# A hybrid decoder layer on one core: mask product in the scores' type, held small products, and the state decode's first part moved

## The chip, the core and the metric

The kernel runs on one core of one Trainium2 chip. The metric is the device time of one execution in microseconds (us). A core has five engines that run at the same time, each through its own queue in order: TensorE (PE, matrix products into PSUM; its weight loads are listed apart as PEld), VectorE (DVE), ScalarE (ACT), GpSimd (POOL) and SyncE (SP, which here issues nearly all DMAs). They wait for one another through semaphores.

## What is computed

One layer, for a prompt of 1024 tokens and for eight decode samples of one token each, with shared weights (width 1024). All arrays are float32.

```
h = x + 0.5 * post1(SwiGLU1(pre1(x)))                 # hidden width 2816
P = pre2(h) @ w_in                                    # 1536 columns group A, 1792 group B
group A: differential attention, 4 heads, 2 maps x 64, causal; samples attend over 512 cached tokens
group B: RWKV-7, 8 heads, state 64 x 64 (value x key) per head
    s = s*w + (s @ -kk)[:, None]*(kk*a) + v[:, None]*k ;  y = s @ r
h = h + post2(concat(A, B) @ w_out)
h = h + 0.5 * post3(SwiGLU2(pre3(h)))
```

Beside the new hidden rows it returns the keys and values, the last projected row and the new RWKV-7 states of prompt and samples. For a sample, group B is a single step of the formula, from a state that comes in (`state_wkv`, 8 samples x 8 heads x 64 x 64).

## The kernel before

**Precision.** A float32 product is made of three products in the rounded type `float32r` (`FR` in the code), which pass the array once: high part by high part, high by low, low by high (`mm3`, line 685). The trunk, the projections, the output product and attention's scores use it. Everything smaller (jobs, decode, probabilities times values, norm sums) is plain float32, which passes the array four times and shows as two matmul records a product; transposes are products with an identity. The causal mask is a third kind: a bfloat16 product `identb` x `negb` (attend, line 265) added to the diagonal block of each score tile, 0 below the diagonal and -1e30 above.

**Phases and halves.** The prompt is cut in two halves of 512 tokens, the samples ride with the first. The trunk (`s_trunk`, line 1021) has four phases: 0 and 1 are the first feed-forward of either half, 2 and 3 the second. Phases 0 and 3 use a scheme with seven block products in place of eight for most of their hidden tiles; phases 1 and 2 (`WIDE`) use 512-column products, except for their first and last hidden tile, which go in chunks of 256 (line 1202: gate and up of chunk 0, then of chunk 1). Each phase ends with down products whose sums DVE adds up (`down`, tile `trunk_xl`).

Between the feed-forwards lies the mixing of each half: projection (`s_project`), RWKV-7 jobs (`s_job`, four a half in two lanes), rotary embedding, attention (`s_prepare`, `s_attend`, `s_finish`; 16 blocks of 128 queries a half in two lanes), output product (`s_out`), norms (`s_stats`, `s_pre`). The mixing of the first half runs beside trunk phase 1, that of the second beside phase 2, so that trunk products fill PE while the mixing waits on DVE and ACT. Phase 3 needs the second half's mixing complete.

**Decode.** `s_decode_a` (1941) does the samples' attention over cached pages, `s_decode_b` (1955) their RWKV-7 step. Both live, one after the other, in one large buffer with the tag `dreg`, which phase 2's first activations use in between and the second half's attention takes over afterwards: `s_mix` (1547) of half 1 waits for the signals of its jobs, of its rotary embedding and for `dec_b`, before `a_buffers`. The trunk's phase 2 waits for `dec_a`. `b_decode` (1993) has a first part (mixing of the eight columns, decay, gates, keys, then a transpose and a store of five row vectors to the DRAM tile `Dd`) and a loop over four pairs of heads: two state loads, then five row tiles, each loaded by two DMAs that broadcast 64-float rows over 64 partitions, products and sums with the state, two state stores. A ring of three row tiles is used.

**Who orders the work.** The body is a set of generators (streams) whose operations are recorded with a price (`price`, 384) and a list of what they depend on. `run` (481) then places them: for each engine it looks at the head of each stream's queue, takes those that could start first, and among them the one with the earliest due time. The order found is written out as the program's order on every engine. The build does this eight times dry, each time with due times that come from the plan before (`latest`, 574), takes the plan with the shortest predicted time and emits it. So an edit of a price, of a rule in `run`, or of one stream gives a new order everywhere. All operations are issued from the one line 323, so the profile's lines don't tell them apart; tiles do. A tile's name begins with its stream: `trunk_`, `proj_`, `job_`, `attn_`, `prep_`, `dec_` and `decb_` for decode, `out_` or `outb_`, `outn_`, `stats_`, `pre_`, `wts_` for the feed-forward's weights, `lin_` for the other weights.

Of the kernel before, what the change touches and what calls it, by code (L numbers as in the profile page):

```python
# [14 lines left out]
FR = mybir.dt.float32r  # L15
# [83 lines left out]
SWAP = 0  # L99
# [6 lines left out]
STARVE = 1  # L106
HUNGER = 0.1
# [108 lines left out]
class Kern:  # L216
# [264 lines left out]
    def run(self):  # L481
        free, held = self.free, self.held
        table, turn = "exp", None
# [4 lines left out]
        while self.streams:  # L488
# [7 lines left out]
            for e in ENGINES:  # L496
                c = []
                for st in self.streams:
                    if st.q[e] and not st.q[e][0].left:
                        o = st.q[e][0]  # L500
                        c.append((max(free[e], o.ready + o.load, held[OTHER[e]] if o.port else lanes[0] if o.dma and e != "gpsimd" else 0.0), st.prio[e] if o.late is None else o.late, o))
                if e == "tensor":
                    starved = not c
                if c:
# [4 lines left out]
                    s, p, o = min((x for x in c if x[0] <= t), key=lambda x: (-round(x[2].columns / x[2].cost / 1000) if dense else self.feeds(x[2]) if hungry else 0, x[1], x[0]))  # L509
# [10 lines left out]
            if o.table is not None and o.table != table:  # L520
                table = o.table
                s += 1.3
            if o.eng == "tensor":
# [41 lines left out]
        self.predicted = max(free.values())  # L565

# [125 lines left out]
    def setup(self):  # L692
# [3 lines left out]
        self.identb = self.T(c, [P, P], "identb", BF)  # L696
# [95 lines left out]
    def stats(self, src, rb, tmp=("sqs", 1), **kw):  # L792

        for k in range(KT):
            if SQP:
                self.square_sum(rb, src[k], k, self.ps2()[:, :rb.shape[-1]], engines=("vector",))
            else:
                self.square_sum(rb, src[k], k, self.tmp(*tmp, rb.shape[-1]), **kw)
# [222 lines left out]
    def s_trunk(self):  # L1021
# [3 lines left out]
        for ph in range(4):  # L1025
# [160 lines left out]
            for gi, grp in enumerate(groups):  # L1186
                for q, f in enumerate(grp):
# [14 lines left out]
                    for fn, c in (((gate, 0), (up, 0), (gate, 1), (up, 1)) if f in (0, NF - 1) else  # L1202
# [46 lines left out]
    def s_tail(self, ph, c, acc, y):  # L1249
# [29 lines left out]
        if ph < 2:  # L1279
# [13 lines left out]
            self.stats(y, self.prb[:, o:o + n], ("sq", 2))  # L1293
# [288 lines left out]
    def b_setup(self, pool):  # L1582
# [6 lines left out]
        self.negb = self.T(c, [P, P], "negb", BF)  # L1589
# [77 lines left out]
    def job(self, pool, i, s, jb):  # L1667
# [143 lines left out]
        for cg in range(4):  # L1811
            nc.sync.dma_start(LT[32 * cg:32 * cg + 32], src)
# [128 lines left out]
    def s_decode_a(self):  # L1941
# [4 lines left out]
        if SWAP:  # L1946
            yield ("wait", "decb")
        yield from self.a_decode()
        if SWAP:
            self.signal("dec_b")  # L1950
        else:
            self.spawn(self.s_decode_b(), "decb", 1, "dec", ahead=8)
        self.signal("dec_a")

    def s_decode_b(self):
        yield ("wait", "proj0")
        yield ("wait", "lead2")
        if SWAP:
            yield ("wait", "setup")
            yield ("wait", "lead1")  # L1960
        take = self.arena(self.T(self.pool, [P, W_DEC], "dreg"))
        yield from self.b_decode(take, take, take(TD, C))
        self.signal("decb" if SWAP else "dec_b")

# [28 lines left out]
    def b_decode(self, m0, m1, tmp):  # L1993
# [3 lines left out]
        ring = [m0(TD, C) for _ in range(3)]  # L1997
        S = m0(TD, C)
        N32 = lambda: m1(4, TD)
        bc = lambda ap: ap.unsqueeze(2).broadcast_to([P, ap.shape[1], TD])  # L2000
        f = lambda ap: ap.rearrange("p i n -> p (i n)")
        X, xt = m1(NB, TD), m1(NB, TD)
# [11 lines left out]
        DV = m1(5, 4, TD)  # L2014
        a, g, t = N32(), N32(), N32()
# [16 lines left out]
        kk, sq = N32(), N32()  # L2032
# [16 lines left out]
        bv = N32()  # L2049
# [5 lines left out]
        V.tensor_tensor(f(bv), f(v), ps[:, :32], ALU.mult)  # L2055

        dv = DV.rearrange("p w i n -> p (w i n)")
        for o, w in ((0, P), (P, 32)):
# [4 lines left out]
            nc.sync.dma_start(self.Dd[o:o + w, :], dr[:w])  # L2063
        yield
        y, sa = N32(), m1(TD)
        at = 0
        kb = lambda ap: ap.unsqueeze(2).broadcast_to([P, TD, C])

        def rows(w, i):
            nonlocal at  # L2070
            B = ring[at % 3]
            at += 1
            for h in range(2):
                src = self.Dd[w * 32 + i * TD:w * 32 + (i + 1) * TD, 64 * h:64 * h + 64]
                nc.sync.dma_start(B[64 * h:64 * h + 64], src.unsqueeze(0).broadcast_to([64, TD, C]))
            return B

        for i in range(4):
            for h in range(2):
                nc.sync.dma_start(S[64 * h:64 * h + 64], I["state_wkv"][0, :, 2 * i + h].rearrange("n v k -> v n k"))  # L2080
            B = [rows(w, i) for w in range(3)]
            yield
            V.tensor_tensor(tmp, S, B[0], ALU.mult)
            B.append(rows(3, i))
            V.tensor_reduce(sa, tmp, AX.X, ALU.add)
            G.tensor_tensor(S, S, B[1], ALU.mult)
            B.append(rows(4, i))
            yield
            V.tensor_tensor(tmp, B[2], kb(sa), ALU.mult)
            V.tensor_tensor(S, S, tmp, ALU.add)  # L2090
            yield
            V.tensor_tensor(tmp, B[3], kb(v[:, i, :]), ALU.mult)
            V.tensor_tensor(S, S, tmp, ALU.add)
            for h in range(2):
                nc.sync.dma_start(self.O[7][0, :, 2 * i + h].rearrange("n v k -> v n k"), S[64 * h:64 * h + 64])
            V.tensor_tensor(tmp, S, B[4], ALU.mult)
            V.tensor_reduce(y[:, i, :], tmp, AX.X, ALU.add)
# [122 lines left out]
    def s_prepare(self, pool, half):  # L2220
# [5 lines left out]
        for rd in range(4 * half, 4 * half + 4):  # L2226
# [121 lines left out]
    def a_decode(self):  # L2348
# [12 lines left out]
        m0, m1 = self.arena(reg[:, 4 * HS + 4 * W:]), self.arena(more)  # L2361
# [162 lines left out]
def hymba_kernel(ctx, tc, I, O, late=None, dry=False):  # L2524
# [10 lines left out]
    K.Dd = DR([160, P], "Dd")  # L2535
# [3 lines left out]
    K.drams = {t.tensor.name: (tuple(t.shape), []) for t in (K.res, K.PTall, K.YMall, *K.Md, *K.Xd, K.Dd, K.Qd, O[3], *K.Ld, *K.Lg, K.Li, K.Lo)}  # L2539
# [27 lines left out]
    if SWAP:  # L2567
        K.spawn(K.s_decode_b(), "decb", 1, "dec", ahead=8)
# [11 lines left out]
_OUTS = [(P, KT, HS), (P, KT, TD), (26, P, NT), (1, 1, TP, 4, P), (P, 4, C), (HS, D), (P, 4, TD), (1, 8, 8, 64, 64)]  # L2580


def layout(inputs):

    f = lambda n: np.asarray(inputs[n])
    given = {n: f(n) for n in _INS if n in ("x_prompt", "cache_k", "cache_v", "state_wkv", "page_table", "w2", "a2", "g2", "ffn1_down", "ffn2_down") or n.startswith("lambda")}
# [5 lines left out]
    for n in ("ffn1_gate", "ffn1_up", "ffn2_gate", "ffn2_up", "w_in", "w_out"):  # L2592
        given[n] = f(n)[0].reshape(KT, P, -1, P).transpose(2, 1, 0, 3)
    given["consts"] = const_table()
# [3 lines left out]
def natural(o):  # L2598
# [8 lines left out]
           ks.transpose(2, 1, 0)[None, :, None], heads(pt[8:12, :, SAMPLE])[None, :, None], states, shift(pt[12:, :, SAMPLE])[None])  # L2607
# [30 lines left out]
```

## Time and profile before

| | us |
|---|---|
| three runs | 2263.15, 2260.83, 2264.13 (median 2263.15) |
| profiled execution, whole | 2263.6 |
| profiled execution, span of its instructions | 2261.8 |
| PE busy | 2204.0 |
| DVE, ACT, POOL busy | 1561.4, 1078.3, 983.4 |

The mean granted clock of PE was 0.994 of full speed. The page lists groups of instructions as `out<-in`. In a timeline row stand the start, the time from the first start to the last end, the engine, the operation, the shapes and the count; in brackets the engine's idle time before it and what ended that. A matmul's listed duration includes its passage through the array, so matmuls overlap; what one costs in a dense stretch is the distance from its start to the next start. In the busy time by stretches, PEclk is the clock granted to PE.

### The profile page before, as it was taken

The page shows a single profiled execution, that of the slowest core. Times are in us where ns is not written, and L with a number is a line of the kernel's source. Part 1 is how long each engine was busy: PE and PEld are TensorE (multiplying, and loading weights), DVE is VectorE, ACT ScalarE, POOL GpSimd, SP SyncE. Part 2 cuts the span into 40 slices and gives each one's busy share as a digit, 9 for nine tenths or more (in the row PEclk, how much of TensorE's full clock was granted, in tenths as well). Part 3 has the DMA queues.
Part 4 walks back from the last instruction along what each step waited for, and adds up shares of the span by engine and source line. Part 5 has one row for each costly group of instructions (what it writes and reads, how often), then busy time and mean ns, then how long its engine had stood idle before and what let it go on. Part 6 is the DMA issues. An engine that isn't in the chain of part 4 may idle for free. (4 is left out here: it accounts for less than half of the span.)

```text
span 2261.8 us, 42336 instructions
## 1 busy us (share of the span) xinstructions
PE 2204.0 (97%) x15671; PEld 1961.9 (87%) x15671; DVE 1561.4 (69%) x3583; ACT 1078.3 (48%) x2222; POOL 983.4 (43%) x817
## 2 busy tenths in 40 slices
PE   8999998999999999999999999999999998999998
PEld 8999998898887777988887777778888988999998
DVE  7758887746766677478656767666877455777775
ACT  6524443644553455343554445333665465544344
POOL 3525554533233575365544334132543254444443
PEclk9999999999999999999999999999999998999999
DMA  7322233444343666555454435358634856443443
GB/s 261 109 94 94 85 103 113 139 148 128 102 121 107 197 185 196 193 177 164 153 197 153 141 94 154 105 146 217 196 108 135 288 175 240 138 135 107 142 141 112
DMA packets 241768, 338.76 MB, mean 150 GB/s; under 512 B 78938, under 2 KB 160282, under 8 KB 241562
## 3 DMA queue, kind: packets, MB, share of 16 engines
q1 hardware_dynamic: 241274, 335.53, 47.3%
q8 instruction: 124, 2.03, 0.4%
q14 instruction: 82, 0.67, 0.1%
q10 hardware_dynamic: 288, 0.52, 0.1%
HBM read 281.01 MB, written 54.98 MB: 149 GB/s over the span
## 5 line engine op out<-in xcount | busy, mean ns | idle before, releaser
L323 PE MATMUL trunk_m<-trunk_xl,wts_w 128*128 128x256 f32 (+2 forms) x2604 | 433.7, 318 | 14.5 <-DVE trunk_xl L323 11.9
L323 PE MATMUL trunk_m<-pre_X,wts_w 128*128 128x512 f32 (+3 forms) x2400 | 430.2, 333 | 9.3 <-ACT wts_w L323 6.5
L323 POOL TENSOR_TENSOR wts_w<-wts_raw,wts_w 128x1024 fp32r<-128x1024 f32 (+2 forms) x154 | 291.9, 1902 | 331.1 <-ACT wts_w L323 284.4
L323 PEld LDWEIGHTS trunk_m<-trunk_xl,wts_w 128*128 128x128 f32 x2604 | 366.2, 190 | 44.4 <-DVE trunk_xl L323 13.5
L323 PEld LDWEIGHTS trunk_m<-pre_X,wts_w 128*128 128x128 f32 x2400 | 353.1, 190 | 49.7 <-ACT wts_w L323 5.9
L323 PE MATMUL trunk_m<-pre_T,wts_w 128*128 128x512 f32 (+3 forms) x1848 | 358.2, 346 | 6.0 <-DVE trunk_xl L323 4.4
L323 ACT CAST wts_w<-wts_raw 128x1024 fp32r<-128x1024 f32 (+3 forms) x299 | 244.9, 834 | 239.7 <-PE trunk_m L323 159.2
L323 PE MATMUL proj_m<-tail_xl,lin_w 128*128 128x256 f32 (+2 forms) x1920 | 327.2, 323 | 0.4 <-POOL lin_w L323 0.4
L323 PEld LDWEIGHTS trunk_m<-pre_T,wts_w 128*128 128x128 f32 x1848 | 288.0, 191 | 43.7 <-issue 2.7
L323 PEld LDWEIGHTS proj_m<-tail_xl,lin_w 128*128 128x128 f32 x1920 | 269.7, 188 | 36.6 <-issue 11.5
L323 DVE TENSOR_TENSOR trunk_xl<-trunk_xl,trunk_m 128x256 f32<-128x256 f32 (+2 forms) x351 | 165.9, 490 | 59.3 <-PE trunk_m L323 57.9
L323 POOL TENSOR_TENSOR lin_w<-lin_raw,lin_w 128x1024 fp32r<-128x1024 f32 x44 | 106.2, 2414 | 199.5 <-ACT lin_w L323 161.7
L323 POOL TENSOR_TENSOR trunk_xl<-trunk_t,trunk_xl 128x512 fp32r<-128x512 f32 (+3 forms) x85 | 92.0, 1084 | 188.3 <-ACT trunk_xl L323 184.7
L323 DVE TENSOR_TENSOR wts_w<-wts_raw,wts_w 128x1024 fp32r<-128x1024 f32 (+3 forms) x115 | 115.7, 1011 | 20.4 <-ACT wts_w L323 18.1
L323 ACT CAST lin_w<-lin_raw 128x1024 fp32r<-128x1024 f32 x52 | 54.5, 1047 | 80.3 <-PE proj_m L323 48.1
L323 ACT CAST wts_w<-wts_lraw 128x512 fp32r<-128x512 f32 x94 | 55.7, 619 | 64.6 <-DMA wts_lraw<-in_ffn_down_dram 36.0
L323 DVE TENSOR_TENSOR trunk_t<-trunk_g,trunk_m 128x512 f32<-128x512 f32 (+2 forms) x75 | 41.9, 559 | 54.0 <-PE trunk_m L323 51.7
L323 PE MATMUL trunk_aux<-trunk_xl,wts_w 128*128 128x256 f32 (+1 forms) x516 | 71.3, 283 | 0.0
L323 PE MATMUL trunk_m<-comb_T,wts_w 128*128 128x260 f32 x540 | 69.7, 283 | 0.0
L323 POOL TENSOR_TENSOR wts_w<-wts_lraw,wts_w 128x512 fp32r<-128x512 f32 x39 | 54.1, 1390 | 35.7 <-ACT wts_w L323 32.3
L323 ACT CAST wts_w<-wts_dec 128x512 fp32r<-128x512 f32 x30 | 17.6, 587 | 107.0 <-DVE wts_dec L323 107.0
L323 PEld LDWEIGHTS trunk_m<-comb_T,wts_w 128*128 128x128 f32 x540 | 66.9, 188 | 0.0
(612 smaller groups left out, 4091.5 us busy)
## 6 DMA issues: line engine op xcount, KB each, us to landing
wts_raw<-in_ffn_gate_dram SPq DMA_DIRECT2D x87, 512.0 KB
wts_raw<-in_ffn_up_dram SPq DMA_DIRECT2D x58, 512.0 KB
lin_raw<-in_w_in_dram SPq DMA_DIRECT2D x52, 512.0 KB
wts_raw<-in_ffn_down_dram SPq DMA_DIRECT2D x56, 384.0 KB
wts_raw<-in_ffn_down_dram SPq DMA_DIRECT2D x29, 512.0 KB
wts_w<-Ld SPq DMA_DIRECT2D x22, 512.0 KB
mix_T<-out_dram SPq DMA_DIRECT2D x36, 256.0 KB
Ld<-wts_w SPq DMA_DIRECT2D x24, 384.0 KB
```

Of the source, the lines that this page charges most:

```text
L323: o = Op(eng, lambda: fn(*a, **k), st)
```

## The change

1. **Mask.** `identb` and `negb` become `float32r`, the type of the scores' products.
2. **Held products.** `price` marks products that pass the array once (`table`; one of `float32r` or bfloat16). In `run`, when the last product was of the one-pass kind, at least one candidate is of that kind and exactly one candidate is not, that one's earliest start is put to 0.5 us after it is ready (`HOLD`). In the planner's timeline a one-pass product that follows another kind in an array of the same shape costs 0.085 us more (`MODE`). `STICK` is 0 and adds nothing.
3. **State decode.** The first part becomes a stream of its own, `decf`, spawned where the attention decode begins and free to run once the first projection is done; it lives in the unused end of `dreg`. It stores gate, bonus term and value to a new DRAM tile `Ed`. `dec_a` waits for it. The second part loads `Ed`, asks for up to four row tiles ahead, and each row tile comes by one DMA in runs of 512 floats (2 KB), since `Dd` is now laid out by half. States are laid out on the host so that they come and go in single DMAs of contiguous rows.
4. **Smaller edits.** Norm sums of phases 2 and 3 square into `E` in place of a buffer `sqs`. The first hidden tile of phases 1 and 2 uses 512-column products. The job's solve matrix and attention's raw keys and queries are loaded by one broadcast DMA in place of four and two.

The core of the diff:

```diff
+HOLD = 0.5
+MODE = 0.085
+STICK = 0
...
+            o.table = f == 1
...
+                if e == "tensor" and HOLD and round_ and any(x[2].table for x in c) and sum(not x[2].table for x in c) == 1:
+                    c = [x if x[2].table else (max(x[0], x[2].ready + HOLD), *x[1:]) for x in c]
...
+                if o.table and not round_:
+                    o.cost += MODE * (size == (t[1] - t[0], t[3] - t[2]))
+                round_ = o.table
...
-        self.identb = self.T(c, [P, P], "identb", BF)
+        self.identb = self.T(c, [P, P], "identb", FR)
-        self.negb = self.T(c, [P, P], "negb", BF)
+        self.negb = self.T(c, [P, P], "negb", FR)
...
-                    for fn, c in (((gate, 0), (up, 0), (gate, 1), (up, 1)) if f in (0, NF - 1) else
+                    for fn, c in (((gate, 0), (up, 0), (gate, 1), (up, 1)) if f == NF - 1 or f == 0 and not wide else
...
-            self.stats(self.staged[c], self.own[c][2][:, :n])
+            self.stats(self.staged[c], self.own[c][2][:, :n], self.E[:, W * c:W * c + n])
...
-        for cg in range(4):
-            nc.sync.dma_start(LT[32 * cg:32 * cg + 32], src)
+        nc.sync.dma_start(LT, src.unsqueeze(0).broadcast_to([4, 32, 1024]))
...
-                    for q in range(2):
-                        nc.sync.dma_start(raw[64 * q:64 * q + 64], src(4 * w + h, t0)[64 * j:64 * j + 64])
+                    nc.sync.dma_start(raw, src(4 * w + h, t0)[64 * j:64 * j + 64].unsqueeze(0).broadcast_to([2, 64, HS]))
```

And the state decode:

```diff
         yield from self.a_decode()
-            self.spawn(self.s_decode_b(), "decb", 1, "dec", ahead=8)
+        yield ("wait", "dec_f")
+        self.spawn(self.s_decode_b(), "decb", 1, "dec", ahead=16)
         self.signal("dec_a")
+    def s_decode_f(self, m0, m1):
+        yield ("wait", "proj0")
+        yield from self.f_decode(m0, m1)
+        self.signal("dec_f")
...
+        V.tensor_copy(gbv[:, 2], v)
+        nc.sync.dma_start(self.Ed, gbv.rearrange("p w i n -> p (w i n)"))
...
-            nc.sync.dma_start(self.Dd[o:o + w, :], dr[:w])
+            nc.sync.dma_start(self.Dd[:, o:o + w, :].rearrange("h p k -> p h k"), dr[:w].rearrange("p (h k) -> p h k", h=2))
...
+        def ask(upto):
+            nonlocal asked
+            while asked < min(upto, 20):
+                i, w = divmod(asked, 5)
+                if w == 0:
+                    nc.sync.dma_start(both[i % 2].rearrange("p n k -> p (n k)"), I["states"][i])
+                B = ring[asked % 4].rearrange("p n k -> p (n k)")
+                src = self.Dd[:, w * 32 + i * TD:w * 32 + (i + 1) * TD, :].rearrange("h n k -> h (n k)")
+                nc.sync.dma_start(B, src.unsqueeze(1).broadcast_to([2, 64, TD * C]))
+                asked += 1
+        ask(4)
...
-            for h in range(2):
-                nc.sync.dma_start(self.O[7][0, :, 2 * i + h].rearrange("n v k -> v n k"), S[64 * h:64 * h + 64])
+            nc.sync.dma_start(self.O[7][i], S.rearrange("p n k -> p (n k)"))
...
+        self.spawn(self.s_decode_f(self.arena(reg[:, at + 512:]), self.arena(more[:, 260:])), "decf", 1, "dec", ahead=8)
```

More of the change, by code (lines that the diff above doesn't have):

```diff
@@ L482, in run @@
         free, held = self.free, self.held
[L483 removed]
+        table, turn, round_ = "exp", None, True
         last = self.last = {}
@@ L508, in run @@
                     hungry = STARVE and starved and e in ("vector", "scalar")
-                    s, p, o = min((x for x in c if x[0] <= t), key=lambda x: (-round(x[2].columns / x[2].cost / 1000) if dense else self.feeds(x[2]) if hungry else 0, x[1], x[0]))
+                    s, p, o = min((x for x in c if x[0] <= t), key=lambda x: (-round(x[2].columns / x[2].cost / 1000) if dense else self.feeds(x[2]) if hungry else 0,
+                                                                              x[1] + STICK * (e == "tensor" and (x[2].table != round_ or self.shape(x[2].tile) != size)), x[0]))
                     if e == "tensor":
@@ L519, in run @@
             self.backlog[o.eng] -= o.cost
-            if o.table is not None and o.table != table:
+            if o.eng == "scalar" and o.table is not None and o.table != table:
                 table = o.table
@@ L565, in run, with shape @@
         self.predicted = max(free.values())
+    @staticmethod
+    def shape(t):
+        return t[1] - t[0], t[3] - t[2]
     @staticmethod
@@ L2062, in b_decode @@
             self.copy(dr[:w], ps[:w, :P])
-            nc.sync.dma_start(self.Dd[o:o + w, :], dr[:w])
+            nc.sync.dma_start(self.Dd[:, o:o + w, :].rearrange("h p k -> p h k"), dr[:w].rearrange("p (h k) -> p h k", h=2))
         yield
-        y, sa = N32(), m1(TD)
-        at = 0
-        kb = lambda ap: ap.unsqueeze(2).broadcast_to([P, TD, C])
[L2069 to L2072, printed above, removed]
-            for h in range(2):
-                src = self.Dd[w * 32 + i * TD:w * 32 + (i + 1) * TD, 64 * h:64 * h + 64]
-                nc.sync.dma_start(B[64 * h:64 * h + 64], src.unsqueeze(0).broadcast_to([64, TD, C]))
-            return B
+    def b_decode(self, take):
+        nc, I = self.nc, self.I
+        V, A, G, mm = nc.vector, nc.scalar, nc.gpsimd, nc.tensor.matmul
+        bc = lambda ap: ap.unsqueeze(2).broadcast_to([P, ap.shape[1], TD])
+        f = lambda ap: ap.rearrange("p i n -> p (i n)")
+        kb = lambda ap: ap.unsqueeze(2).broadcast_to([P, TD, C])
+        ring = [take(TD, C) for _ in range(4)]
+        both = [take(TD, C) for _ in range(2)]
+        tmp, gbv, y, sq, sa = take(TD, C), take(3, 4, TD), take(4, TD), take(4, TD), take(TD)
+        g, bv, v = (gbv[:, j] for j in range(3))
+        nc.sync.dma_start(gbv.rearrange("p w i n -> p (w i n)"), self.Ed)
+        asked = 0
+        def ask(upto):
[9 more added lines that the diff above has]
+        ask(4)
+        yield
@@ L2078, in b_decode @@
         for i in range(4):
[L2079 to L2082, printed above, removed]
+            S = both[i % 2]
+            B = [ring[(5 * i + w) % 4] for w in range(5)]
             V.tensor_tensor(tmp, S, B[0], ALU.mult)
-            B.append(rows(3, i))
+            ask(5 * i + 5)
             V.tensor_reduce(sa, tmp, AX.X, ALU.add)
@@ L2538, in hymba_kernel @@
     K.Li, K.Lo = DR([26, P, KT, P], "Li"), DR([KT, P, KT, P], "Lo")
-    K.drams = {t.tensor.name: (tuple(t.shape), []) for t in (K.res, K.PTall, K.YMall, *K.Md, *K.Xd, K.Dd, K.Qd, O[3], *K.Ld, *K.Lg, K.Li, K.Lo)}
+    K.drams = {t.tensor.name: (tuple(t.shape), []) for t in (K.res, K.PTall, K.YMall, *K.Md, *K.Xd, K.Dd, K.Ed, K.Qd, O[3], *K.Ld, *K.Lg, K.Li, K.Lo)}
     K.c2 = K.const
@@ L2593, in layout @@
         given[n] = f(n)[0].reshape(KT, P, -1, P).transpose(2, 1, 0, 3)
+    given["states"] = f("state_wkv")[0].reshape(TD, 4, P, C).transpose(1, 2, 0, 3).reshape(4, P, TD * C)
     given["consts"] = const_table()
```

58 lines of the change are left out of this document (24 added, 34 removed).

## The prediction

> **What bounds the kernel now.** I read the page first, then the busy time by stretches, then the timeline of each stretch in which TensorE (PE) is not full.
>
> ```profile
> span 2261.8 us, 42336 instructions
> ## 1 busy us (share of the span) xinstructions
> PE 2204.0 (97%) x15671; PEld 1961.9 (87%) x15671; DVE 1561.4 (69%) x3583; ACT 1078.3 (48%) x2222; POOL 983.4 (43%) x817
> ```
>
> PE is busy 97% of the span and every other engine 69% or less, so what counts is work removed from PE or idle time removed on PE. Of idle time there are only 2261.8 - 2204.0 = 57.8 us. This profiled execution took 2263.6 us (its span and 1.8 us around it), 0.45 us more than the median 2263.15 of the three runs shown. My sum is made against 2263.6 and ends 0.45 lower for the median. About 0.2%, 4.5 us, is what a measurement of this kernel can tell from no change.
>
> ```profile
> core 0: us, PE busy (x) PEld busy (x) DVE busy (x) ACT busy (x) POOL busy (x), PEclk, DMA share, GB/s
> 372.00:396.00 24.00, 18.80 (x128) 18.30 (x127) 13.86 (x34) 9.76 (x21) 11.72 (x13) 0.86 0.15 44
> 1110.00:1165.00 55.00, 53.03 (x301) 45.74 (x301) 41.31 (x63) 32.76 (x63) 36.05 (x39) 1.00 0.61 210
> 1530.00:1580.00 50.00, 50.00 (x217) 40.10 (x217) 31.87 (x45) 15.08 (x18) 16.09 (x9) 1.00 0.89 222
> 1580.00:1760.00 180.00, 178.29 (x986) 147.76 (x985) 132.44 (x284) 111.93 (x299) 76.10 (x46) 1.00 0.50 150
> 1760.00:1836.00 76.00, 75.99 (x511) 69.65 (x509) 31.21 (x44) 38.38 (x65) 28.59 (x30) 1.00 0.84 286
> 1836.00:1890.00 54.00, 40.36 (x293) 37.40 (x292) 35.80 (x68) 33.36 (x66) 28.52 (x41) 0.91 0.36 112
> ```
>
> The rows are where the trunk passes from phase 0 to 1, from 1 to 2, and four pieces of the second half's mixing ahead of phase 3. One stretch stands out: 1836 to 1890, where PE has 40.36 of 54 us, 13.6 us idle, and a granted clock of 0.91. It is the largest single piece of the 57.8 us, and it is the joint between phases 2 and 3.
>
> **Why that joint is empty, and what fills it.** In the second half the trunk of phase 2 is PE's filler while the mixing runs: jobs, then attention, then the output product, then the norms that make phase 3's input.
>
> ```profile
> 1526.18 1.02 PE L323 MATMUL job_aux<-bset_sg,bset_g 128*128 128x512 f32 x2
> ...
> 1582.82 0.48 PE L323 MATMUL attn_aux<-mix_T 128*128 128x320 f32 x2
> ```
>
> The last job's last product is at 1526, attention's first at 1583. In between PE is full (50.00 of 50), but with filler alone. What holds attention is the state decode (`decb`), whose tile attention's buffers take over:
>
> ```profile
> L323 SPq DMA_DIRECT2D decb_dreg<-Dd x40: 573/628/1772, 1490.7 to 1562.1; - x40
> L323 DVE TENSOR_TENSOR decb_dreg<-decb_dreg x34: 184/690/2729, 1457.0 to 1580.2; 128x512 f32<-128x512 f32 x24, 128x32 f32<-128x32 f32 x9, 128x112 f32<-128x112 f32 x1
> ...
> L323 DVE TENSOR_REDUCE decb_dreg<-decb_dreg x8: 677/686/687, 1498.6 to 1570.3; 128x8 f32<-128x512 f32 x8
> ```
>
> It starts at 1457, loads its first row at 1490.7, loops until 1571 and ends at 1580. The filler burnt in that gap is missing at the end:
>
> ```profile
> 1832.10 2.76 PE L323 MATMUL outb_m<-outb_T,lin_w 128*128 128x256 f32 x22
> ```
> ```profile
> 1870.59 0.48 DVE L323 SCALAR_TENSOR_TENSOR pre_T<-pre_sq,init_cols,pre_T 128x256 fp32r<-128x256 f32 x1 [0.29 <-ACT pre_T L323]
> ...
> 1872.51 7.48 PE L323 MATMUL trunk_m<-trunk_xl,wts_w 128*128 128x256 f32 x45 [7.14 <-DVE trunk_xl L323]
> ```
>
> The output product ends at 1835, and the norms behind it keep DVE and ACT until 1871: a chain of 36 us. In it the trunk is already in its last down products, whose sums wait on DVE behind those norms, so PE waits 7.14 us at a stretch. After that wait 45 products of 256 columns take 7.48 us, 166 ns each, against 120 ns at 773 us (below): 2.0 us more at the lower clock. The Trainium skill (TensorE: Matmul & The Clock Gate, part 1) says that PE's clock falls to half after an idle window of some 3.4 us; the 7.14 us wait and the 0.91 agree.
>
> **The change part by part.**
>
> *State decode.* Its first part (from the load of the eight columns to the rows' store to DRAM, 1457 to 1490) moves ahead of the first half's attention, into 740 to 800 us. Every instruction of it still counts, but PE fills the place it leaves with trunk products, so this is zero in sum; it adds two small DMAs (store and reload of gate, bonus and value) and one small copy, and its few issues on SP pass between the loads of cached pages, which have slack there as decode of attention is waited for only at phase 2's start. Its result is due some 300 us later, so the new wait for it stands in nobody's way. The second part then starts where the first part starts now: 34 us earlier. Its loop takes (1571 - 1491) = 80 us for 20 rows of 256 KB, four states in and four out, 7.3 MB. With one issue a row in place of two (628 ns each, 40 to 20: 12.6 us of SP) and 2 KB packets, its bytes at the 222 GB/s of 1530:1580 take 33 us; DVE's 32 large operations, at 0.69 us, take 22. So the loop takes 33 to 80 us; I take 50. Decode's end then is 1457 + 50 + 10 = 1517, at the worst 1547, and attention is let go by the last job at 1527 or by 1547: 33 to 50 us earlier than 1580. SP may stand at a row's issue until DVE frees one of four buffers, with the trunk's weight loads queued behind it; the same waits stand there now with three buffers, so I count nothing.
>
> *What that is worth.* Filler worth 33 to 50 us is left for the 36 us chain. If all is covered, the joint is left with what a joint without such a chain has: 24 - 18.80 = 5.2 us idle at phase 0 to 1, or 55 - 53.03 = 2.0 at 1 to 2. I take the larger, since phase 2's tail has the same DVE sums. Gain at full cover: 13.6 - 5.2 + 2.0 = 10.4 us.
>
> *Small products wait for company.* When the last product was one of the trunk's kind, a trunk product is at hand, and exactly one small product stands ready, it may be put up to 0.5 us later, and its followers (DVE and ACT of that job or block) with it. This is an order fixed when the kernel is built: on the chip PE waits for no clock, it does trunk products meanwhile. First, what a change of kind costs on PE, together with the mask:
>
> ```profile
> 770.39 0.22 PE L323 MATMUL attn_aux<-mix_X 128*128 128x128 f32 x1
> 770.45 2.77 PE L323 MATMUL trunk_m<-trunk_xl,wts_w 128*128 128x512 f32 x11
> 773.06 0.28 PE L323 MATMUL attn_aux<-mix_X 128*128 128x256 f32 x1
> 773.18 0.22 PE L323 MATMUL attn_aux<-mix_X,mix_X 128*128 128x128 f32 x1
> ...
> 773.60 0.23 PE L323 MATMUL attn_aux<-bset_negb,init_identb 128*128 128x128 bf16 x1
> 773.64 0.36 PE L323 MATMUL attn_m<-mix_X 128*128 128x256 f32 x1
> 773.84 2.02 PE L323 MATMUL trunk_m<-trunk_xl,wts_w 128*128 128x512 f32 x8
> ...
> 780.46 0.60 PE L323 MATMUL prep_cb<-init_ident,mix_T 128*128 128x128 f32 x4
> 780.81 2.58 PE L323 MATMUL trunk_m<-trunk_xl,wts_w 128*128 128x512 f32 x10
> 783.23 4.33 PE L323 MATMUL trunk_m<-pre_T,wts_w 128*128 128x512 f32 x18
> ```
>
> I read starts, not durations. Four transposes take 780.81 - 780.46 = 0.35 us, and the ten trunk products behind them 2.42 in place of 10 x 0.233 = 2.33: 0.44 in all, 0.11 a transpose. The 0.09 seen on the first trunk product is what the last transpose's slot lacks (0.35 is three slots and a bit); I see no charge for the change of kind beyond it, so a merge of two groups of full-array products saves nothing. Where the array shape changes too, merging may save some; I have no row for a count, and bound all of it between 0 and 4 us (40 merges at 0.1), taking 0. The Trainium skill (TensorEngine Tiling (Array Packing), Key Properties) says that a change of tiling mode drains TensorE; by it the saving would be nearer 4.
>
> The price is in the chains. A job's chunk steps follow one another:
>
> ```profile
> 1497.93 0.40 PE L323 MATMUL job_aux<-bset_Sd,mix_T 128*128 128x128 f32 x2
> ...
> 1500.25 0.38 PE L323 MATMUL job_aux<-bset_Sd,mix_T 128*128 128x128 f32 x2
> ```
>
> One step is 2.3 us, and the wait can make it 2.8. By the code a lane has two jobs with some 25 such returns to PE each, and attention eight blocks a lane with five: 90 returns at 0 to 0.5 us, 0 to 45 us. Often two lanes stand ready or the product was no hurry; I take 15 us. So attention and output end some 45 - 15 = 30 us earlier in place of 45, and cover 30 of the 36 us: gain about 8.5 us instead of 10.4.
>
> *Mask.* The bf16 mask at 773.60 holds the array 0.04 us, and the 256-column product behind it takes 0.20 in place of the 0.12 from 773.06 to 773.18: 0.12 in all. The 128-column product of the scores' dtype at 770.39 takes 0.06, and the eleven behind it 2.61 in place of 11 x 0.233 = 2.56: 0.11 in all. So 64 masks (32 blocks, two maps each) save 64 x 0.01 = 0.6 us; bounds -1 and +4. The Trainium skill (same page as above, Fast Weight Load) speaks against it: weights of 128 columns load fast unless they are FP32. By an estimate from its column rule (128/1.2 ns at half saved, 53 ns) 64 masks would cost 3.4 us more if nothing hid the loads.
>
> *First products of phases 1 and 2 in 512 columns.* Now gate and up go in two chunks, and a bank is wanted every 2.8 us:
>
> ```profile
> 386.10 3.06 PE L323 MATMUL trunk_m<-pre_T,wts_w 128*128 128x256 f32 x24
> ...
> 391.18 5.07 PE L323 MATMUL trunk_m<-pre_T,wts_w 128*128 128x256 f32 x28 [2.02 <-DVE trunk_xl L323]
> ```
>
> After one chunk (24 products) PE waits 2.02 us for DVE to empty the other bank. A 512-column product chain runs 24 x 0.233 = 5.6 us before it wants that bank, past 391.18, so these 2.0 us go. At phase 2 no such wait is listed: 0.
>
> *The rest, at nothing.* One broadcast load for two or four (job solve, attention's raw loads) takes issues off SP, which PE waits for nowhere in these rows; if it waited, they would gain. Squares into `E` in place of their one buffer: ACT has the cover of 48% use. Every order is planned anew; I allow 3 us each way.
>
> *Sum.* 8.5 + 0.6 + 2.0 = 11.1; 2263.6 - 11.1 = 2252.5, the median 0.45 lower: **2252 us**.
>
> **The rivals.**
>
> *Held products lengthen the chains past what decode gives (slower).* If each of the 90 returns pays 0.5 us, 45 us eat the whole lead; with decode's end at 1547 (33 us) the output would end 12 us later than now. From the point where the wait adds more than decode gives, each us is one more at the joint, since the filler runs out before: 12 - 2.6 = 9.4 us, 2263.15 + 9.4 = 2272.5. For it: the last job's steps have PE to themselves, one small product at a time. Against: two lanes run for most of the time. Chance 0.11.
>
> *The joint stays as it is (no difference).* The 7.14 us wait is on the trunk's own sums on DVE, and the transposes of the rows and the blocks for phase 3 still fall there. Then only 0.6 and 2.0 are gained: 2260.5. For it: 372:396 has 5.2 us idle with no mixing about. Chance 0.16.
>
> *A change of kind costs what it seems to.* If the 0.09 on the first trunk product is a real charge, and a quarter of the returns by the code (8 jobs x 25 and 32 blocks x 5, 360) is merged, 90 x 0.09 = 8 us more go: 2244. The starts above speak against it. Chance 0.12.
>
> *The packets do nothing.* If decode's loop keeps its 80 us, its first part still leaves: that is the 1547 above, within the forecast.
>
> **How the numbers follow.** The forecast (2245 to 2258) has 0.61. The range takes in full cover, 4 us of merges, 3 of re-planning and most of the third rival (down to 2241), and the second rival with 3 us (2264); left out are the first rival and the third's edge, under 0.2. Faster by over 0.2% (below 2258.6): 0.61 + 0.12 and none of the rest, 0.73. Within: 0.16. Slower: 0.11.
>
> **What would show it.** Right: `decb` with its first row before 1460 and its end before 1530 (or the last job's end as the gate), attention's first product by 1550, the stretch between output's end and phase 3's first product with under 7 us idle and a clock near 1, no wait at 389, mask slots as before. Wrong: attention no earlier, or the output no earlier because job steps went from 2.3 to 2.8 us; or an unchanged 7 us wait for DVE at the joint; or a PE busy sum that fell by over 5 us, which would mean that changes of kind cost something.

## The result, and the profile after

The changed kernel takes 2498.62 us (median of four runs, 2497.67 to 2500.14) against 2263.64 for the kernel before on the same chip: a ratio of 1.104 with an interval of [1.102, 1.106]. It is 235 us slower; 2252 had been forecast. The page of its profile begins:

```profile
span 2497.2 us, 41941 instructions
## 1 busy us (share of the span) xinstructions
PE 2258.1 (90%) x15575; PEld 2010.0 (80%) x15575; DVE 1538.5 (62%) x3576; ACT 1078.7 (43%) x2219; POOL 993.1 (40%) x820
```

PE does about the same products and was idle for 239.1 us in place of 57.8. Its busy time rose too, by 54, at a mean granted clock of 0.948 where it had 0.994, and 181 + 54 is the whole difference of the spans. The busy time by stretches of the changed kernel says where (columns as before: the five engines, PE's granted clock, DMA share, GB/s):

```profile
700.00:1000.00 300.00, 236.70 (x1252) 190.82 (x1249) 172.66 (x453) 111.24 (x286) 120.99 (x82) 0.88 0.43 130
1400.00:1900.00 500.00, 367.75 (x2081) 292.22 (x2080) 224.88 (x637) 169.66 (x399) 135.36 (x86) 0.84 0.33 103
1664.00:1670.00 6.00, 4.75 (x19) 3.59 (x17) 0.09 (x1) 0.41 (x2) 4.63 (x3) 0.80 0.13 50
1796.00:1799.00 3.00, 3.00 (x15) 2.48 (x14) 2.17 (x6) 1.80 (x5) 1.05 (x1) 1.00 0.13 52
```

And of the kernel before, the same two long stretches:

```profile
700.00:1000.00 300.00, 293.45 (x1712) 242.79 (x1712) 200.15 (x442) 141.60 (x332) 165.58 (x120) 1.00 0.60 182
1400.00:1900.00 500.00, 481.30 (x2946) 403.03 (x2945) 320.35 (x671) 256.18 (x564) 194.06 (x159) 0.99 0.58 172
```

In the mixing of either half PE loses 63.3 and 132.3 us where it lost 6.6 and 18.7, and runs at 0.88 and 0.84 of full clock. No other engine is busier, and the DMA engines are less busy than before. The two short rows point at the loads: for microseconds on end the DMA share is 0.13, two engines of sixteen, at some 50 GB/s. In those moments only one kind of transfer is under way. SP's timeline in the state decode:

```profile
1555.27 0.33 SPq L325 DMA_DIRECT2D decb_dreg<-Ed  x1
1555.63 0.43 SPq L325 DMA_DIRECT2D decb_dreg<-in_states_dram  x1
1556.11 9.45 SPq L325 DMA_DIRECT2D decb_dreg<-Dd  x4
1565.66 5.07 SPq L325 DMA_DIRECT2D wts_raw<-in_ffn_up_dram  x1
1570.83 0.68 SPq L325 DMA_DIRECT2D decb_dreg<-Dd  x1
1571.56 6.21 SPq L325 DMA_DIRECT2D decb_dreg<-in_states_dram  x1
1577.87 0.59 SPq L325 DMA_DIRECT2D decb_dreg<-Dd  x1
1578.51 5.22 SPq L325 DMA_DIRECT2D wts_raw<-in_ffn_down_dram  x1
```

Row loads of 256 KB follow each other, and soon every other issue, of whatever load comes next, stands for 5 to 6 us: 256 KB at 50 GB/s are 5.2 us. The trunk's own weight loads (`wts_raw`) stand in that line. The same in the groups of issues by tile (ns: shortest, median, longest), the changed kernel first, then the kernel before:

```profile
L325 DVE TENSOR_TENSOR decb_dreg<-decb_dreg x28: 185/692/696, 1563.7 to 1698.8; 128x512 f32<-128x512 f32 x24, 128x32 f32<-128x32 f32 x4
L325 SPq DMA_DIRECT2D decb_dreg<-Dd x20: 507/1254/5629, 1556.1 to 1663.1; - x20
...
L325 SPq DMA_DIRECT2D bset_la<-out_dram x11: 532/4126/6326, 764.3 to 1863.7; - x11
```
```profile
L323 SPq DMA_DIRECT2D bset_la<-out_dram x20: 422/567/597, 728.1 to 1663.9; - x20
```

Fewer issues, but the median one takes 4.1 us in place of 0.57. The waits of the changed kernel (us in total, times, longest):

```profile
DVE decb_dreg L325 <- DMA decb_dreg<-Dd: 68.8, 15, 7.3
...
ACT mix_T L325 <- DMA mix_T<-out_dram: 48.7, 11, 5.6
...
PE job_aux L325 <- ACT mix_T L325: 34.8, 7, 10.4
```

The first two are row tiles and raw tiles. PE's own wait at the jobs hangs on both, since DVE and ACT take their work in order. Two of its seven waits in the timeline:

```profile
1677.70 0.69 DVE L325 TENSOR_TENSOR decb_dreg<-decb_dreg 128x512 f32<-128x512 f32 x1 [5.03 <-DMA decb_dreg<-Dd]
1678.31 0.34 DVE L325 SCALAR_TENSOR_TENSOR bset_Sd<-job_aux,job_ec,init_bones 128x128 f32<-128x128 f32 x1
...
1678.69 0.42 ACT L325 COPY mix_T<-job_aux 64x64 f32<-64x64 f32 x2 [14.14 <-DVE bset_Sd L325]
...
1679.17 0.80 PE L325 MATMUL job_aux<-bset_Sd,mix_T 128*128 128x128 f32 x2 [10.42 <-ACT mix_T L325]
...
1694.81 0.62 ACT L325 CAST mix_T<-bset_la 128x512 fp32r<-128x512 f32 x1 [4.57 <-DMA bset_la<-out_dram]
1695.45 0.43 ACT L325 COPY mix_T<-job_aux 64x64 f32<-64x64 f32 x2
...
1695.93 0.80 PE L325 MATMUL job_aux<-bset_Sd,mix_T 128*128 128x128 f32 x2 [8.35 <-ACT mix_T L325]
```

At 1677 the job's step on DVE (`bset_Sd`) stands behind a row tile, at 1694 its copy on ACT stands behind a raw tile, and PE waits 10.4 and 8.4 us for them. The decode, by the first line of the groups above, ends at 1699 (before: 1580). On PE's timeline attention's first product of half 1 follows at 1724 (1583) and the output's last ones at 2041 to 2044 (1835):

```profile
1724.21 0.76 PE L325 MATMUL attn_aux<-mix_T 128*128 128x320 f32 x2 [3.27 <-ACT mix_T L325]
...
2041.40 2.77 PE L325 MATMUL outb_m<-outb_T,lin_w 128*128 128x256 f32 x22
```

**Theory.** The loads that became "one broadcast load in place of two or four" have an outermost count of 2 (rows, raws: `[2, 64, ...]`) or 4 (solve: `[4, 32, 1024]`), and run on that many DMA engines. A rival: held products and the new order stretch the chains.

### The profile page after: what moved, and what is told of

Read it like the earlier page. It is cut to its first block, busy times and chain, and to the rows that moved or that the text cites. A ratio compares the mean times of both kernels' runs of the same rounds, so it can differ in the third digit from the quotient of the medians.

```text
span 2497.2 us, 41941 instructions
## 1 busy us (share of the span) xinstructions
PE 2258.1 (90%) x15575; PEld 2010.0 (80%) x15575; DVE 1538.5 (62%) x3576; ACT 1078.7 (43%) x2219; POOL 993.1 (40%) x820
## 3 DMA queue, kind: packets, MB, share of 16 engines
q8 instruction: 123, 2.02, 0.3%
## 5 line engine op out<-in xcount | busy, mean ns | idle before, releaser
L325 PE MATMUL trunk_m<-pre_X,wts_w 128*128 128x512 f32 (+3 forms) x2352 | 439.8, 342 | 11.4 <-ACT wts_w L325 6.0
L325 PEld LDWEIGHTS trunk_m<-pre_X,wts_w 128*128 128x128 f32 x2352 | 359.9, 194 | 57.2 <-ACT wts_w L325 6.0
L325 PE MATMUL trunk_m<-pre_T,wts_w 128*128 128x512 f32 (+3 forms) x2016 | 389.8, 346 | 0.9 <-DMA wts_w<-Lg 0.5
L325 PEld LDWEIGHTS trunk_m<-pre_T,wts_w 128*128 128x128 f32 x2016 | 312.5, 191 | 42.9 <-issue 1.9
L325 PEld LDWEIGHTS proj_m<-tail_xl,lin_w 128*128 128x128 f32 x1920 | 277.5, 193 | 37.6 <-issue 7.5
L325 DVE TENSOR_TENSOR trunk_xl<-trunk_xl,trunk_m 128x264 f32<-128x264 f32 (+2 forms) x343 | 165.0, 493 | 57.5 <-PE trunk_m L325 56.2
L325 POOL TENSOR_TENSOR trunk_xl<-trunk_t,trunk_xl 128x512 fp32r<-128x512 f32 (+3 forms) x79 | 83.7, 1062 | 167.4 <-ACT trunk_xl L325 167.2
L325 PE MATMUL trunk_aux<-trunk_xl,wts_w 128*128 128x264 f32 (+1 forms) x570 | 78.5, 284 | 0.0
L325 PEld LDWEIGHTS trunk_aux<-trunk_xl,wts_w 128*128 128x128 f32 x570 | 72.6, 189 | 0.0
L325 ACT CAST trunk_xl<-trunk_t 128x512 fp32r<-128x512 f32 (+3 forms) x96 | 46.2, 482 | 40.5 <-DVE trunk_t L325 39.6
```

Source lines behind the costliest of these rows:

```text
L325: o = Op(eng, lambda: fn(*a, **k), st)
```

## The experiments

**1. The broadcast loads split back** (all else of the change kept, the 2 KB runs too):

```diff
-nc.sync.dma_start(raw, src(...)[64*j:64*j+64].unsqueeze(0).broadcast_to([2, 64, HS]))
+for q in range(2):
+    nc.sync.dma_start(raw[64*q:64*q+64], src(...)[64*j:64*j+64])
-nc.sync.dma_start(LT, src.unsqueeze(0).broadcast_to([4, 32, 1024]))
+for cg in range(4):
+    nc.sync.dma_start(LT[32*cg:32*cg+32], src)
-nc.sync.dma_start(B, src.unsqueeze(1).broadcast_to([2, 64, TD * C]))
+for h in range(2):
+    nc.sync.dma_start(B[64*h:64*h+64], src[h:h+1].broadcast_to([64, TD * C]))
```

> The changed kernel with its three broadcast loads (row tiles of the state decode, attention's raw queries and keys, the job's solve matrix) issued as separate loads again, 2, 2 and 4 for one, 2 KB runs kept. Narrow loads (the theory: such a load moves at about 50 GB/s, DMA share 0.13, and holds SP and all that is queued behind it): the 235 us go, 2250 to 2265 us. Held products (the rival: chains lengthened by products that wait 0.5 us): the three loads matter little, 2450 to 2500 us. New order (second rival: the plan itself is worse): above 2300 us too, with PE waits spread over all stretches.

Measured: 2260.59 us (ten runs, 2247.59 to 2263.76), ratio 0.998 [0.997, 1.000]. All 235 us are gone with these three lines, and either kernel moves the same 338.8 MB. The groups by tile and the stretches of this kernel:

```profile
L325 SPq DMA_DIRECT2D decb_dreg<-Dd x40: 444/587/1914, 1470.5 to 1517.5; - x40
L325 DVE TENSOR_TENSOR decb_dreg<-decb_dreg x28: 181/691/2315, 1474.7 to 1534.5; 128x512 f32<-128x512 f32 x24, 128x32 f32<-128x32 f32 x4
...
L325 SPq DMA_DIRECT2D bset_la<-out_dram x20: 465/588/2147, 745.7 to 1631.9; - x20
```
```profile
372.00:396.00 24.00, 21.40 (x120) 18.97 (x119) 16.32 (x37) 10.19 (x19) 11.77 (x13) 0.93 0.15 46
...
1475.00:1515.00 40.00, 37.23 (x256) 28.37 (x255) 28.94 (x44) 11.95 (x20) 15.30 (x11) 0.91 0.86 231
...
1836.00:1890.00 54.00, 53.83 (x374) 49.73 (x373) 28.06 (x51) 26.84 (x48) 21.02 (x26) 1.00 0.48 151
```

The issues are at 0.59 us again, and the decode's loop (1475 to 1515) moves 231 GB/s on 0.86 of the engines. The last row is the joint of the prediction: 53.83 of 54 us where the kernel before had 40.36. Yet the time is that of before, which experiments 6 to 12 take up.

**2. Held products off, the broadcast loads kept** (`HOLD = 0`, `MODE = 0`).

> The changed kernel without the held products and without the price of a change of kind; all broadcast loads stay. Narrow loads: stays at 2470 to 2520 us. Held products: back to 2250 to 2290 us. New order: something in between, since every order is planned anew.

Measured: 2508.15 us, ratio 1.108 [1.106, 1.110]. It isn't the holding: without it the loss is no smaller.

**3. The kernel before, with raw and solve loads as broadcasts, and nothing else of the change.**

> The kernel before with nothing but the two broadcast loads of attention's raw tiles and the job's solve matrix, one load for two and for four. Narrow loads: 48 raw tiles of 256 KB at 50 GB/s are 5 us each, 12 in a row on a half's path at the least, and 8 solve matrices of 512 KB: slower by 60 to 200 us, 2320 to 2460 us. Held products and new order: within 10 us of 2263 us, since neither rule nor decode is changed.

Measured: 2445.78 us, ratio 1.081 [1.079, 1.083]. Two lines make a tuned kernel 184 us slower, with no new order asked for by anything else. (The order of the whole is planned anew here too, but orders alone moved the time by some 27 us, as experiments 6 to 12 show, not by 184.) Behind a solve load (issued at 1521) its stretch shows the other share:

```profile
1522.00:1528.00 6.00, 5.64 (x39) 4.18 (x37) 1.38 (x2) 0.38 (x1) 0.00 (x0) 1.00 0.24 70
```

0.24, four engines of sixteen.

**4. Rows alone split back.**

> The changed kernel with only the state decode's row tiles loaded in two halves each; raw tiles and solve matrix stay broadcast. Narrow loads: the part of the loss between 1555 and 1700 us goes (20 row tiles at 5 us are 100 us, part of it hidden by trunk products), 2400 to 2460 us. Held products: no change, 2480 to 2510 us.

Measured: 2432.37 us, ratio 1.075 [1.073, 1.077].

**5. Rows and solve split back, raw loads left broadcast.**

> The changed kernel with its row loads and job solve loads split, and attention's raw loads left as one broadcast of two. The kernel before with raw and solve broadcasts lost 184 us. Theory of the narrow load: a load whose outermost count is 2 moves about 50 GB/s, so 48 of 256 KB hold SP's queue about 5 us each, and most of the 184 is theirs: 2390 to 2440 us. Rival: the solve loads (8 of 512 KB at about twice the rate) hold up the job chain, which the state decode and attention wait for, and carry more than half: 2300 to 2350 us.

Measured: 2376.38 us, ratio 1.050 [1.049, 1.052]. (The expectation counts 48 raw loads; the loops give 16 in the first half and 24 in the second, 40.) With this the bill can be written, each row the difference of two of these kernels:

| loads made wide | time after | worth | loads | each |
|---|---|---|---|---|
| none (the change) | 2498.6 | | | |
| rows | 2432.4 | 66 | 20 | 3.3 |
| and solve | 2376.4 | 56 | 8 | 7.0 |
| and raw | 2260.6 | 116 | 40 | 2.9 |

A row or raw load moves for 5.2 us and costs about 3; a solve load has twice the bytes and costs 7. The rival (most of it in the solve loads) falls, though the time lies between the two ranges expected, 14 us below the nearer end of the theory's; raw loads carry the most, but only by their number. (Each of these kernels also has an order of its own; what that is worth comes next, and each row is uncertain by it. Split in another sequence, the loads could share the bill otherwise.)

**6 to 9. What is left of the change.** The split kernel shows the gains at the joint and at the first hidden tile, and yet its time can't be told from that of before. So parts of it were taken away: holding (`HOLD = 0`, `MODE = 0`); the mask back in bfloat16 (`identb`, `negb`); both, with the old order of the first hidden tile as well, so that of the change mainly the early decode remains; and holding off with the bfloat16 mask.

> The split version (the change with its three broadcast loads as two, four and two loads again, 2260.6 us) without the held products: HOLD and MODE are 0. Theory H, that holding small products makes the new short stalls of the split version (3.8 us at 1274 and its neighbours, 279.3 us of 290 in 1165 to 1455 where the kernel before had 285.6): 2243 to 2255 us, and that stretch back at 284 or more. Rival N, that any new order of the planner's brings stalls of that size somewhere: 2255 to 2265 us, with that stretch mended and others worse. Rival P, that the holding is worth something on TensorE: slower than the split version by 3 us or more.

> The split version with the mask product in bf16 as before. By the slots of the profile before (0.12 us against 0.11, 64 masks) it would be 0.6 us slower than the split version, 2261 us, so nothing that can be told apart. Rival: the change of kind costs 0.09 us at each of 64 masks and another 64 times behind, so it is 6 to 12 us slower, 2266 to 2272. Rival N as for the run without holding: the mask's kind also enters the planner's prices, so the order changes, and the time moves by up to 5 us either way for that alone.

> The split version with HOLD and MODE 0, the mask in bf16 and the old order of the first f: what is left of the change is the state decode's first part early with its rows in 2 KB runs, and the squares in the stats' own buffer. By the prediction's own steps this part was worth 8.5 to 10.4 us through the covered joint: 2251 to 2254 us. Rival N: the order changes and gives it back, 2256 to 2265 us. If the decode alone is slower than 2265, the new stalls are its own.

> Split version, mask in bf16, HOLD and MODE 0. It closes the square of the two switches: hold and scores' type gave 2260.6 us, hold and bf16 2233.8, no hold and scores' type 2247.2. If the two act by themselves (the mask's type costs 27 us, holding 13), this is 2220 us. If each only shuffles the planner's order (rival N), it lies among the others with no rule, 2233 to 2255.

Measured, and beside each PE's idle time in 1165 to 1455, the stretch of the second half's projection and job chains:

| split kernel | us | ratio | idle 1165-1455 |
|---|---|---|---|
| held, mask in bfloat16 | 2233.8 | 0.988 [0.987, 0.990] | 2.6 |
| not held | 2247.2 | 0.993 [0.992, 0.994] | 3.0 |
| not held, mask in bfloat16 | 2249.2 | 0.994 [0.993, 0.996] | 4.1 |
| early decode mainly | 2253.2 | 0.995 [0.994, 0.997] | 6.0 |
| held, mask in the scores' type | 2260.6 | 0.998 [0.997, 1.000] | 10.7 |

(The kernel before is idle for 4.4 us in that stretch.) Experiment 6, not held, came out as its theory on holding had it, and experiment 8, early decode mainly, as the prediction's steps had it; experiment 7, held with the mask in bfloat16, lies some 22 us below every range expected. The square of the two switches shows that such hits say little. The mask in bfloat16 is 27 us faster with holding and 2 us slower without. No cost of a mask does that. Holding costs 13 us with one mask and gains 15 with the other. If the two acted by themselves, the third row would be 2220. (The ten runs of the last row spread over 16 us, more than any other's, so the 27 and the 13 are rough.)

**10 to 12. Order, or substance?** The mask's type enters the planner's price (107 ns against 56), so it changes the order of everything. One kernel keeps the fastest one's order and has the mask in the scores' type on the chip (the price alone stays bfloat16's), one changes `HOLD` from 0.5 to 0.4, one takes back the first hidden tile's order.

> The split version with bf16 mask (2233.8 us) and its order kept, each product and load where it was; only the mask product is in the scores' type on the chip again. Theory N: what parted 2260.6 from 2233.8 is the order that came out of another price for the mask, so this stays at 2232 to 2236 us, 0.6 us from it by the slots. Rival: the scores' type is itself dear at the mask, and this goes to 2250 to 2262.

> The split version with bf16 mask and HOLD 0.4 in place of 0.5: a change of a price by 0.1 us that says the same thing. Theory N: the order is shuffled and the time moves by 5 us or more from 2233.8, to 2238 to 2258. Rival, that 2233.8 comes from holding as such: it stays within 4 us, 2230 to 2238.

> The split version with bf16 mask, with the old order of the first f. By the prediction's step the new order is worth 2.0 us (the wait of 2.0 us at 389): 2236 us. Theory N: a shuffle again, 2238 to 2258. Rival: the new order is worth more than its step, 2245 and over with the wait at 389 back and no other stretch worse.

Measured: 2234.87 us, 0.988 [0.986, 0.990]; 2260.93 us, 0.999 [0.998, 1.000]; 2246.76 us, 0.993 [0.992, 0.994]. The first says that the mask's type does nothing that can be told in the time (1.1 us inside overlapping intervals): the order did it. The second says how much an order is worth: a tenth of a microsecond in a planner's constant costs 27 us, a little more than expected. The third costs 13 us, of which its own place shows the 2.0 of the prediction's step (PE idle for 5.4 us in 250 to 500, against 3.4); other stretches are worse too, such as 1540 to 1700 (3.9 against 1.0), so its rival, a new order worth more than its step, isn't borne out. The same stretch in the fastest kernel and in that with `HOLD` 0.4:

```profile
1165.00:1455.00 290.00, 287.45 (x1961) 227.23 (x1960) 187.51 (x564) 136.99 (x260) 101.99 (x61) 1.00 0.47 139
```
```profile
1165.00:1455.00 290.00, 281.77 (x1919) 220.64 (x1918) 176.65 (x500) 132.34 (x251) 92.48 (x56) 0.99 0.43 128
```

5.7 us of the difference are here. The two profiles differ by 30.2 us in all, 10.4 of it PE's idle time and 19.8 its busy time, for the same 15575 products; why these took longer wasn't traced.

**A version that beats both kernels:** the change with its three broadcast loads split and the mask in bfloat16, 2233.81 us (2229.14 to 2238.14), 1.2% below the kernel before. It is the best of seven orders, and not shown to be better by its mask.

## Why the prediction was wrong

**The step that failed** is "The rest, at nothing": "One broadcast load for two or four (job solve, attention's raw loads) takes issues off SP, which PE waits for nowhere in these rows; if it waited, they would gain." It counted issues and not the engines that one issue uses. It cost 172 us (experiments 4 to 1), and the same error in the decode, "with one issue a row in place of two ... its bytes at the 222 GB/s", cost 66. The rows read for SP were those of loads issued in two or four parts. How fast one load in their place would move had no row in the trace of before, and should have had bounds of its own in place of the 222 GB/s of other loads. The prediction even saw "the trunk's weight loads queued behind" a row on SP, and counted nothing because "the same waits stand there now": SP's waits in that stretch of the kernel before were 1.6 us in all, and in the changed one a single weight load's issue stands for 5.

The Trainium skill states this rule (DMA: Bandwidth & Descriptors, Rules for kernel authors): the slowest dimension of a DMA's patterns sets how many engines it uses, and a leading zero-stride broadcast of c copies confines it to at most c. The runs agree: 0.13 of the engines for c = 2, 0.24 for c = 4. The prediction weighed rules for TensorE and none for the loads, and left out the one that gave the other sign.

**Steps that held**, seen once the loads are split. Decode: the loop and its end were forecast as 60 us; in the first split kernel the decode's DVE work runs from 1474.7 to 1534.5. It all lies later than forecast, though: the first row comes at 1470.5, not before 1460, and the last job's last product at 1543, not 1527. Attention is let go by the last job, as forecast. On the timeline of the same kernel

```profile
385.81 12.46 PE L325 MATMUL trunk_m<-pre_T,wts_w 128*128 128x512 f32 x53
...
1542.71 1.02 PE L325 MATMUL job_aux<-bset_sg,bset_g 128*128 128x512 f32 x2
1548.68 0.48 PE L325 MATMUL attn_aux<-mix_T 128*128 128x320 f32 x2
```

attention starts 6 us behind the last job's product, at 1549 ("by 1550") and 34 us earlier than before. The output's last product starts 31 us earlier (1804), and 30 were forecast; that is luck in part, for in the other split kernels it is 25 to 57.

The joint has 0.2 us idle in 1836 to 1890 at a full clock, where under 7 was asked. But idle time came back elsewhere: 53.4 us in the whole profile against 57.8, with 6.3 more in 1165 to 1455 and 3.0 more in 1455 to 1540. That a filled joint shortens the kernel by what it held is not seen in this order.

The first hidden tile: its 512-column products run from 385.81 with no wait in 53 of them, so the 2.02 us at 391 are gone; 372 to 396 has 2.6 us less idle time (21.40 against 18.80), where 2.0 was forecast.

The mask: experiments 7 and 10 have the same order, so their 64 masks can be compared one by one, start to start. The median mask holds the array for 39 ns in bfloat16 and 60 in the scores' type, the product behind it for 314 and 282: 11 ns less together, 0.7 us in all, where 0.6 was forecast. That is too little to see in the time, and the 53 ns a mask that the prediction estimated against it isn't there.

**Held products.** They lengthen the chains in the first half. The transposes of its jobs, in the kernel before, in the fastest one (held) and in that of experiment 9 (not held):

```profile
L323 PE MATMUL job_aux<-init_ident,mix_X x176: 218/218/328, 505.4 to 757.1; 64*64 64x64 f32 x128, 128*128 128x128 f32 x48
```
```profile
L325 PE MATMUL job_aux<-init_ident,mix_X x176: 216/218/329, 505.2 to 769.8; 64*64 64x64 f32 x128, 128*128 128x128 f32 x48
```
```profile
L325 PE MATMUL job_aux<-init_ident,mix_X x176: 218/218/328, 501.9 to 748.5; 64*64 64x64 f32 x128, 128*128 128x128 f32 x48
```

From first to last 264.6 us held, 246.6 not held: 18 us. But the 15 us of the prediction were taken for the second half, on the way to attention. The steps of its jobs in the same three kernels:

```profile
L323 PE MATMUL job_aux<-bset_Sd,mix_T x64: 270/275/377, 1317.1 to 1505.2; 128*128 128x128 f32 x64
```
```profile
L325 PE MATMUL job_aux<-bset_Sd,mix_T x64: 270/274/378, 1299.6 to 1499.6; 128*128 128x128 f32 x64
```
```profile
L325 PE MATMUL job_aux<-bset_Sd,mix_T x64: 270/275/377, 1309.2 to 1508.4; 128*128 128x128 f32 x64
```

That is 200.0 us held and 199.2 not held; with the other mask it is 205.3 and 202.2. From attention's first product to the output's last, held products make no longer a way either (260.8 us against 276.7, and 255.2 against 256.1). So holding costs 1 to 3 us in these jobs where 15 were taken for jobs and attention, and the first rival, held products that eat up the lead, falls. In all four the jobs' steps take longer than the 188.1 of the kernel before, held or not. That the 15 nearly fit the first half is luck.

The third rival, that a change of kind costs what it seems to, has as its sign a PE busy sum lower by over 5 us. Holding lowers that sum by 9.9 us with the mask in bfloat16 (2186.8 against 2196.7) and raises it by 8.8 with the other (2205.3 against 2196.5), so no such cost is shown; one of a few microseconds stays open.

**A term mis-sized:** "Every order is planned anew; I allow 3 us each way." The seven split kernels with orders of their own, which do all but the same work, lie between 2233.8 and 2260.9: 13.6 us each way. Their median is 2249.2 and their mean 2250.2, near the forecast of 2252, which single orders miss by up to 18 us; and the kernel before is one order too, so how much of those 12 to 14 us is the change and how much is the draw stays open. The effect of any single small edit of this kernel under some 27 us can't be told from that of its order by one build.

## What to carry to other kernels

Before two DMAs become one, look at the outermost count of the new pattern: a broadcast written as `[2, 64, n]` saved an issue of 0.6 us and cost some 3 us at each load: it ran on two engines, and loads issued behind it waited. In the trace this looked like idle engines everywhere, a low DMA share near 2/16 or 4/16 (0.13, 0.24), and issues that last microseconds. Where a planner lays out the whole program, build several orders of any variant before an effect of 1% is given to the edit; holding the order fixed (experiment 10) is the clean way to price one operation.

## What the runs showed of the hardware

A load with an outermost count of 2 kept the DMA share at 0.13 and moved 47 to 53 GB/s; behind one of 4 the share was 0.24, at 70 GB/s. The DMA activity of the changed kernel in 40 slices from 1656 to 1670 (first row the share in tenths):

```profile
DMA  9397973111111111111991111111111111111111
GB/s 205 135 328 293 339 205 94 47 47 47 47 53 53 47 47 53 53 47 47 398 357 53 53 53 47 47 53 53 47 53 53 47 47 53 53 47 47 53 53 47
```

Other loads pass at up to 398 GB/s in a slice or two, then two engines work alone. That SP's issues behind such loads stand for 4 to 6 us, although fourteen engines are idle, had not been expected: the narrow load is paid not only by whoever needs its bytes, but by loads queued behind it. Why the issue stands so long isn't shown by any run here.
